# Opening of a diffusion layer on one core: x loaded in half token tiles, the first modulation weights in quarters, and the modulation turned and summed by 128x2 products

## The chip, the cores and the metric

The kernel runs on one core of one Trainium2 chip. The metric is the device time of one execution in microseconds, as the median of several. Engines are named as in the profile: PE is TensorE (its weight loads are PEld), DVE is VectorE, ACT is ScalarE, POOL is GpSimd, SP is the engine that issues most transfers.

## The reference, cut to what matters

The layer normalises 256 latent tokens x and 256 context tokens ctx (D = 2048 channels), modulates them with a scale and a shift that come from a conditioning vector, projects them, and runs neighbourhood attention and a gated linear attention on the projections. What the change touches is the modulation:

```python
mod = jax.nn.silu(c) @ w_mod[l] + b_mod[l]
shift, scale, gate = jnp.split(mod[:, None, :], 3, axis=-1)
mod_c = jax.nn.silu(c_ctx) @ w_mod[l] + b_mod[l]
shift_c, scale_c, gate_c = jnp.split(mod_c, 3, axis=-1)
h = _layer_norm(x) * (1.0 + scale) + shift
h_c = _layer_norm(ctx) * (1.0 + scale_c) + shift_c
aq, ak, av, az, bq, bk, bv, bz, bg, mga, mgb = _split_cols(h @ w_in[l])
```

There are two conditioning vectors (c for the latent tokens, c_ctx for the context), so every channel has two scales and two shifts. All arithmetic is float32; a projection is made of three products of rounded halves (high x high, low x high, high x low).

## The kernel before

The channels are cut into 16 steps kt of 128. The opening (up to about 141 us) makes h for all steps and, at the same time, the projection ak for the first 7 groups of 128 columns (`kps`, `kp2`, names kp0 to kp6). It goes like this:

- SP loads the conditioning vector (cv), four token tiles `rows` of 128 tokens x 2048 channels (1 MB each), and for every step kt the modulation weights `wm{kt}_0` and `wm{kt}_1` (1 MB each; 8 blocks of 128 input channels x 256 outputs, which are 128 scales and 128 shifts) and the key weights `r_ak` (448 KB). `fetch` chains them in this order; `fetch_kt(kt)` issues a step's three. Two steps are fetched at the start, the others from `prepare`, when buffers come free: those of the modulation weights have the tag k8, with 8 buffers.
- PE turns the token tiles (products xt with the identity `ident`, 4 of 128x128 for each evacuation by ACT), and DVE takes mean and variance (`bn_stats`). From these come rsn, and two PE turns and copies make `stat`, with which DVE normalises a step's xt (`normalise`, two instructions).
- `modulate(kt, q)`: 8 products of 32 x 256 per half q, into the PSUM tile gp. The conditioning vectors stand in columns 0 and 1 of 32 (`scp`), and each of the four groups of 32 PSUM partitions collects a quarter of the input channels. So gp holds, in 128 rows, four partial sums of two vectors (rows 32g and 32g + 1) for 256 outputs.
- `activate(kt)`: gp is copied to SBUF (gs; ACT for step 0, DVE for the others), its two halves are turned by PE (L294, into the upper half of gp's bank), so that the outputs lie on the partitions, DVE sums the four groups (the reduction at L297) and adds the bias (L300). The result, `mds`, has a scale and a shift for both token kinds. ACT then makes h rounded (`hl`, L306, two instructions), DVE the same in full precision (h32, L307) and the low half (L308).
- `split_ak` rounds the key weights on ACT (h_ak) and makes their low half on DVE (l_ak, L151).
- Then the 21 kp products of a step: 7 groups x (h_ak with high h, l_ak with high h, h_ak with low h).

A scheduler of the framework sets the order on each engine, from the order of the code, `issue_after` links and its own estimate of times; each engine works through its own list strictly in that order. After the opening, PE goes on with the queries of the first heads (qp), the values and the rest of the layer.

Of the kernel before, what the change touches and what calls it, by code (L numbers as in the profile page):

```python
# [8 lines left out]
F32 = mybir.dt.float32  # L9
# [3 lines left out]
ALU = mybir.AluOpType  # L13
AX = mybir.AxisListType
PSUM = bass.MemoryType.PSUM

P = 128
D = 2048
KT = 16
T = 256  # L20
# [69 lines left out]
def tile_backbone_layer(  # L90
# [21 lines left out]
    nc = tc.nc  # L112
    const = ctx.enter_context(tc.tile_pool(name="const", bufs=1))
# [9 lines left out]
    def k8(shape, name, dt=F32):  # L123
        return work.tile(shape, dt, tag="k8", name=name, bufs=8)
# [4 lines left out]
    def k2(shape, name, dt=F32):  # L129
        return work.tile(shape, dt, tag="k2", name=name, bufs=5)  # L130

    def acc(name):
        return ps.tile([P, 512], F32, tag="acc", name=name, bufs=4)
# [7 lines left out]
    def tiny(shape, name, bufs=4):  # L141
        return small.tile(shape, F32, tag=name, name=name, bufs=bufs)

    def mm(o, a, b, start, stop):
        return nc.tensor.matmul(o, a, b, start=start, stop=stop).ins  # L145
# [24 lines left out]
    ident = const.tile([P, P], F32, name="ident")  # L170
    make_identity(nc, ident)
    rows = hpool.tile([P, 8, D], F32, tag="hl", name="rows")

    def log_exp_after(act):
        with tc.issue_after(act.ins):
            nc.scalar.preload_act_table_set("natural_log_exp_and_others")
# [4 lines left out]
    def fetch(dst, src):  # L181
        with tc.issue_after(queued[-1]) if queued else nullcontext():
            queued.append(nc.sync.dma_start(dst, src).ins)

    def behind(ins):
        return tc.issue_after(ins) if ins is not None else nullcontext()

    wms, raws = {}, {}

    def fetch_kt(kt):  # L190
        wms[kt] = [k8([P, 8, T], f"wm{kt}_{q}") for q in range(2)]
        for q in range(2):
            fetch(wms[kt][q][:], wmod[kt, q])
        raws[kt] = stream.tile([P, 1024], F32, tag="raw", name=f"r_ak_{kt}", bufs=4)
        fetch(raws[kt][:, : P * K0], wak[kt])

# [1 line left out]
    fetch(cv[:], cvec)  # L198
    xts = [k8([P, 4, 512], f"xt{i}") for i in range(4)]
    for i in range(4):  # L200
        fetch(rows[:, i, :], xin[i])
    for kt in range(2):
        fetch_kt(kt)
    bm = const.tile([P, KT, 2, 2], F32, name="bm")
    nc.scalar.dma_start(bm[:], bmod)
    nc.gpsimd.tensor_scalar(bm[:, :, 0, :], bm[:, :, 0, :], 1.0, None, ALU.add)
    sc = const.tile([P, KT, 2], F32, name="sc")
    log_exp_after(nc.scalar.activation(sc[:], cv[:], AF.Sigmoid))
    nc.gpsimd.tensor_tensor(out=sc[:], in0=sc[:], in1=cv[:], op=ALU.mult)
    scp = k2([P, KT, 32], "scp")  # L210
# [20 lines left out]
    for i in range(4):  # L231
        cols = slice(P * i, P * i + P)
        for c in range(4):
            tp = acc(f"xt{i}_{c}")
            for k in range(4):
                kt = 4 * c + k
# [15 lines left out]
    gps, made, pend, last_mm, gs_ins = {}, {}, {}, [None], []  # L252
# [31 lines left out]
    def activate(kt):  # L284
        gp = gps[kt]
        gs = k2([P, T], f"gs{kt}")
        if kt:
            with behind(made[0][1] if kt == 1 else None):
                nc.vector.tensor_copy(gs[:], gp[:, :T])
        else:  # L290
            gs_ins.append(nc.scalar.copy(gs[:], gp[:, :T]).ins)
            split_ak(0)
        for c in range(2):
            t = nc.tensor.transpose(gp[:, T + P * c : T + P * c + P], gs[:, P * c : P * c + P], ident[:])  # L294
        last_mm[0] = t.ins
        md = mds[:, :, :, kt]
        nc.vector.tensor_reduce(  # L297
            md, gp[:, T:].rearrange("p (c g m) -> p c m g", c=2, g=4)[:, :, 0:2, :], AX.X, ALU.add
        )
        nc.vector.tensor_tensor(out=md, in0=md, in1=bm[:, kt], op=ALU.add)  # L300
        h32 = k2([P, 2, T], f"h32_{kt}")
        for s in range(2):
            x = xts[kt // 4][:, kt % 4, T * s : T * s + T]
            m, b = mds[:, 0, s, kt : kt + 1], mds[:, 1, s, kt : kt + 1]
            with behind(pend[0][2] if kt == 0 else None):
                cast = nc.scalar.activation(hhi[:, s, kt, :], x, AF.Identity, scale=m, bias=b)  # L306
            nc.vector.tensor_scalar(h32[:, s, :], x, m, b, ALU.mult, ALU.add)  # L307
        sub = nc.vector.tensor_tensor(  # L308
            out=hlo[:, :, kt, :], in0=h32[:], in1=hhi[:, :, kt, :].bitcast(F32), op=ALU.subtract
        )  # L310
        made[kt] = cast.ins, sub.ins

    def split_ak(kt):
        hi = stream.tile([P, 1024], F32R, tag="hi", name=f"h_ak_{kt}")
        lo = stream.tile([P, 1024], F32R, tag="lo", name=f"l_ak_{kt}")
        n = P * K0
        if kt == 0:
            with behind(gs_ins[0]):
                cast = nc.scalar.copy(hi[:, :n], raws[0][:, :n]).ins
            pend[0] = hi, lo, cast  # L320
            return
        split(hi[:, :n], lo[:, :n], raws[kt][:, :n], made[max(kt - 1, 1)])
        pend[kt] = hi, lo
# [11 lines left out]
    with tc.high_priority(offset=60):  # L335
        normalise(0)
        activate(0)
# [6 lines left out]
    def prepare(kt):  # L344
        if kt + 1 < KT:
            fetch_kt(kt + 1)
        normalise(kt)
        modulate(kt)
        activate(kt)
        split_ak(kt)  # L350

    for kt in range(KT):
# [3 lines left out]
        for p in range(K0):  # L356
# [3 lines left out]
            c = slice(P * p, P * p + P)  # L360
# [244 lines left out]
    for g in range(3):  # L605
        q = k8([P, 2, 2, 2, T], f"q{g}", F32R)
# [13 lines left out]
    q = k8([P, 2, 2, 2, T], "q3", F32R)  # L620
# [284 lines left out]
    for i in range(2):  # L905
        s = slice(4 * i, 4 * i + 4)
# [113 lines left out]
    while steps or waiting:  # L1020
        gate_step()
    log_exp_after(sig)
    tail = hpool.tile([P, 8, D], F32, tag="hl", name="tail")
    fin, gb, zs, zt0 = tail[:, 0:4], tail[:, 4], (tail[:, 5], tail[:, 6]), tail[:, 7]
# [42 lines left out]
    for g in range(NC - 1):  # L1067
        ops = [acc(f"wo{g}_{t}") for t in range(2)]
        for k in range(0, KT, 2):
# [5 lines left out]
            for t in range(2):  # L1075
                for i in range(2):
                    c = slice(512 * i, 512 * i + 512)
# [53 lines left out]
    op = acc("wol_0")  # L1131
# [3 lines left out]
    for i in range(2):  # L1135
        op = acc(f"wol_1{i}")
# [9 lines left out]
    r, q = tiny([P, 1], "rr"), tiny([P, 1], "rt")  # L1146
# [109 lines left out]
```

## Time and profile before

| | |
|---|---|
| time, median of 3 runs | 1223.0 us (1222.77 to 1223.78) |
| the profiled execution | 1226.52 us |
| its span | 1224.8 us, granted clock 0.998 |
| PE busy | 1200.0 us (98%) |
| DVE busy | 772.7 us (63%) |
| ACT busy | 542.6 us (44%) |
| wm transfers | 32 of 1024 KB, 9.1 us from issue to landing (median) |
| r_ak transfers | 16 of 448 KB, 9.4 us |
| rows transfers | 4 of 1024 KB, 8.5 us |

The span is the profiled execution from its first to its last instruction; the device time lies around it. A busy PE is not a PE at its peak: matmuls are pipelined, so a record's duration is longer than its distance to the next. The chain of waits goes back from the last instruction to whatever released it, step by step; only work on it sets the end. The windows give busy time of each engine in a stretch of the span and the share and rate of the 16 transfer engines.

### The profile page before, as it was taken

The page shows a single profiled execution, that of the slowest core. Times are in us where ns is not written, and L with a number is a line of the kernel's source. Part 1 is how long each engine was busy: PE and PEld are TensorE (multiplying, and loading weights), DVE is VectorE, ACT ScalarE, POOL GpSimd, SP SyncE. Part 2 cuts the span into 40 slices and gives each one's busy share as a digit, 9 for nine tenths or more (in the row PEclk, how much of TensorE's full clock was granted, in tenths as well). Part 3 has the DMA queues.
Part 4 walks back from the last instruction along what each step waited for, and adds up shares of the span by engine and source line. Part 5 has one row for each costly group of instructions (what it writes and reads, how often), then busy time and mean ns, then how long its engine had stood idle before and what let it go on. Part 6 is the DMA issues. An engine that isn't in the chain of part 4 may idle for free.

```text
span 1224.8 us, 16303 instructions
## 1 busy us (share of the span) xinstructions
PE 1200.0 (98%) x6233; PEld 991.0 (81%) x6233; DVE 772.7 (63%) x1154; ACT 542.6 (44%) x768; POOL 64.0 (5%) x87
## 2 busy tenths in 40 slices
PE   6999999999999999999999999999999999999997
PEld 5666798989788887888888888888888888888885
DVE  7655677777658676356433376766566665665677
ACT  5322445555545354253533364444444444454340
POOL 1000100000010210002000000000000000000111
PEclk9999999999999999999999999999999999999999
DMA  9998457868632444534445667677676767657661
GB/s 376 417 409 310 133 179 222 260 183 266 226 120 86 138 139 136 190 123 153 158 175 187 220 232 239 230 235 237 240 237 236 238 240 239 231 182 284 222 207 69
DMA packets 77054, 263.45 MB, mean 215 GB/s; under 512 B 8920, under 2 KB 8936, under 8 KB 71856
## 3 DMA queue, kind: packets, MB, share of 16 engines
q1 hardware_dynamic: 73616, 256.69, 60.6%
q0 software_dynamic: 2928, 5.16, 1.8%
q8 instruction: 49, 0.80, 0.3%
q10 hardware_dynamic: 432, 0.56, 0.1%
q14 instruction: 29, 0.24, 0.1%
HBM read 247.66 MB, written 10.52 MB: 211 GB/s over the span
## 4 chain that ended last, share of the span: by engine, by line
PE 78%; DVE 8%; DMA 8%; ACT 3%; issue 2%; POOL 0%; SPq 0%; DVEq 0%; ACTq 0%; POOLq 0%
PE bz L145 7%; PE mgb L145 7%; PE pb L145 7%; PE mga L145 7%; PE o L145 7%; PE g L145 7%; PE kp L145 6%; PE bk L145 5%; PE pa L145 4%; PE bq L145 3%; PE wo L145 3%; PE az L145 3%; PE va L145 2%; DMA sb<-mods 2%; PE gp L145 2%
## 5 line engine op out<-in xcount | busy, mean ns | idle before, releaser
L145 PE MATMUL va<-h_av,hl 128*128 128x352 f32 x384 | 95.7, 325 | 0.9 <-DVE both_aq L391 0.9
L145 PE MATMUL kp<-hl,h_ak 128*128 128x512 f32 x256 | 87.2, 408 | 2.2 <-ACT hl L306 2.2
L151 DVE TENSOR_TENSOR l_wv<-r_wv,h_wv 128x1024 fp32r<-128x1024 f32 x32 | 39.2, 1225 | 72.9 <-ACT h_wv L149 72.8
L145 PE MATMUL o<-h_wv,gt 128*128 128x512 f32 x256 | 83.9, 390 | 0.7 <-ACT gt L149 0.5
L145 PE MATMUL bk<-hl,h_bk 128*128 128x512 f32 x256 | 80.8, 392 | 0.7 <-ACT kf L680 0.7
L145 PE MATMUL bz<-h_bz,hl 128*128 128x512 f32 x256 | 80.7, 392 | 0.0
L145 PE MATMUL mgb<-h_mgb,hl 128*128 128x512 f32 x256 | 79.8, 390 | 0.0
L145 PE MATMUL mga<-h_mga,hl 128*128 128x512 f32 x256 | 79.5, 389 | 0.0
L145 PE MATMUL pb<-h_pb,hl 128*128 128x512 f32 x256 | 79.4, 389 | 0.0
L145 PE MATMUL g<-ah,hr 128*128 128x512 f32 x256 | 79.0, 390 | 0.0
L145 PEld LDWEIGHTS va<-h_av,hl 128*128 128x128 f32 x384 | 67.1, 188 | 2.1 <-DVE both_aq L391 1.2
L149 ACT CAST h_wv<-r_wv 128x1024 fp32r<-128x1024 f32 x32 | 33.6, 1050 | 71.3 <-DMA r_wv<-in_wst 71.3
L151 DVE TENSOR_TENSOR l_pb<-r_pb,h_pb 128x1024 fp32r<-128x1024 f32 x32 | 39.2, 1225 | 39.9 <-ACT h_pb L149 39.9
L145 PEld LDWEIGHTS kp<-hl,h_ak 128*128 128x128 f32 x256 | 48.3, 191 | 19.4 <-issue 4.9
L145 PE MATMUL va<-l_av,hl 128*128 128x352 f32 x192 | 61.7, 321 | 0.0
L151 DVE TENSOR_TENSOR l_mgb<-r_mgb,h_mgb 128x1024 fp32r<-128x1024 f32 x32 | 39.2, 1225 | 30.1 <-ACT h_mgb L149 29.9
L145 PEld LDWEIGHTS o<-h_wv,gt 128*128 128x128 f32 x256 | 48.0, 188 | 11.5 <-ACT gt L149 0.9
L145 PEld LDWEIGHTS bk<-hl,h_bk 128*128 128x128 f32 x256 | 48.1, 188 | 11.3 <-ACT kf L680 1.1
L151 DVE TENSOR_TENSOR l_mga<-r_mga,h_mga 128x1024 fp32r<-128x1024 f32 x32 | 39.2, 1224 | 27.5 <-ACT h_mga L149 27.5
L145 PEld LDWEIGHTS mga<-h_mga,hl 128*128 128x128 f32 x256 | 48.1, 188 | 10.0
L145 PEld LDWEIGHTS pb<-h_pb,hl 128*128 128x128 f32 x256 | 48.1, 188 | 9.9
L145 PEld LDWEIGHTS bz<-h_bz,hl 128*128 128x128 f32 x256 | 48.1, 188 | 9.9
(332 smaller groups left out, 2962.7 us busy)
## 6 DMA issues: line engine op xcount, KB each, us to landing
wm<-in_wmod SPq DMA_DIRECT2D x32, 1024.0 KB, 9.1
hr<-hrows SPq DMA_DIRECT2D x32, 512.0 KB, 4.4
r_wv<-in_wst SPq DMA_DIRECT2D x32, 512.0 KB, 3.6
r_bz<-in_wst SPq DMA_DIRECT2D x32, 512.0 KB, 4.2
wg<-in_wgate SPq DMA_DIRECT2D x64, 256.0 KB, 3.6
r_mga<-in_wst SPq DMA_DIRECT2D x32, 512.0 KB, 4.2
r_mgb<-in_wst SPq DMA_DIRECT2D x32, 512.0 KB, 3.3
r_pb<-in_wst SPq DMA_DIRECT2D x32, 512.0 KB, 3.3
```

Of the source, the lines that this page charges most:

```text
L145: return nc.tensor.matmul(o, a, b, start=start, stop=stop).ins
L149: cast = nc.scalar.copy(hi, src)
L151: sub = nc.vector.tensor_tensor(out=lo, in0=src, in1=hi.bitcast(F32), op=ALU.subtract)
```

## The change

Three edits. The four x transfers become eight of 4 KB rows (half the channels of a token tile each), and the first step's two modulation weight transfers become four. A 128x2 selector `sel` is made once, by a DVE reduction of the identity: its column m has ones in the rows 32g + m. And the two turns of gs against the identity become two products of gs with `sel`, whose results are the two columns of a half already summed over the four groups, so that the reduction on DVE goes and the bias is added straight from PSUM.

```diff
+    sel = const.tile([P, 2], F32, name="sel")
+    nc.vector.tensor_reduce(
+        sel[:], ident[:].rearrange("p (g c) -> p c g", g=4)[:, 0:2, :], AX.X, ALU.add
+    )
...
         for q in range(2):
-            fetch(wms[kt][q][:], wmod[kt, q])
+            for i in range(0, 8, 8 if kt else 4):
+                s = slice(i, i + (8 if kt else 4))
+                fetch(wms[kt][q][:, s], wmod[kt, q][:, s])
...
     for i in range(4):
-        fetch(rows[:, i, :], xin[i])
+        for c in range(0, D, 1024):
+            fetch(rows[:, i, c : c + 1024], xin[i][:, c : c + 1024])
...
         for c in range(2):
-            t = nc.tensor.transpose(gp[:, T + P * c : T + P * c + P], gs[:, P * c : P * c + P], ident[:])
-        last_mm[0] = t.ins
+            t = mm(gp[:, T + 2 * c : T + 2 * c + 2], gs[:, P * c : P * c + P], sel[:], True, True)
+        last_mm[0] = t
         md = mds[:, :, :, kt]
-        nc.vector.tensor_reduce(
-            md, gp[:, T:].rearrange("p (c g m) -> p c m g", c=2, g=4)[:, :, 0:2, :], AX.X, ALU.add
-        )
-        nc.vector.tensor_tensor(out=md, in0=md, in1=bm[:, kt], op=ALU.add)
+        sums = gp[:, T : T + 4].rearrange("p (c m) -> p c m", c=2)
+        nc.vector.tensor_tensor(out=md, in0=sums, in1=bm[:, kt], op=ALU.add)
```

It also moves instructions, since the scheduler orders them anew. First PE, from the turn of step 13 (gp13) to the first half of gp14; a row is a line of the code, the operation, what it writes and reads, its shape, and how many. Before:

```order
L294 MATMUL gp13_1054<-ident_77,gs13_1071 128x128 x2
L145 MATMUL kp45_300<-hl_247,l_ak_12_1022 128x512
L145 MATMUL kp45_300<-hl_247,h_ak_12_1021 128x512 x2
L145 MATMUL kp45_300<-hl_247,l_ak_12_1022 128x512
L145 MATMUL kp45_300<-hl_247,h_ak_12_1021 128x512
L145 MATMUL kp6_301<-hl_247,h_ak_12_1021 128x512
L145 MATMUL kp6_301<-hl_247,l_ak_12_1022 128x512
L145 MATMUL kp6_301<-hl_247,h_ak_12_1021 128x512
L145 MATMUL gp14_1116<-wm14_0_1046,scp_112 32x256 x8
L145 MATMUL kp0_296<-hl_247,h_ak_13_1083 128x512
```

After, on PE, from the pair of step 13 to the same half of gp14:

```order
L145 MATMUL gp13_1049<-sel_83,gs13_1066 128x2 x2
L145 MATMUL kp6_308<-hl_255,l_ak_12_1017 128x512
L145 MATMUL kp6_308<-hl_255,h_ak_12_1016 128x512
L145 MATMUL kp0_303<-hl_255,h_ak_13_1077 128x512
L145 MATMUL kp1_304<-hl_255,h_ak_13_1077 128x512
L145 MATMUL kp2_305<-hl_255,h_ak_13_1077 128x512
L145 MATMUL kp0_303<-hl_255,l_ak_13_1078 128x512
L145 MATMUL kp1_304<-hl_255,l_ak_13_1078 128x512
L145 MATMUL kp2_305<-hl_255,l_ak_13_1078 128x512
L145 MATMUL gp14_1110<-wm14_0_1041,scp_120 32x256 x8
```

Eight products of step 12 and half a gp stood between the turn of step 13 and its first kp product; now two products do, and the half gp stands behind six products of step 13. The second half of a gp has moved behind in the same way. Between the pair and the first kp product of its own step there are now 9 products for kt=9, 5 for kt=10, then 2, 3, 2, 3 and 2 for kt=11 to 15; up to kt=8 there is little change.

DVE in the same step, before:

```order
L289 COPY gs13_1071<-gp13_1054 128x256
L297 TENSOR_REDUCE mds_116<-gp13_1054 128x4
L151 TENSOR_TENSOR l_ak_13_1084<-r_ak_13_988,h_ak_13_1083 128x896
L300 TENSOR_TENSOR mds_116<-mds_116,bm_105 128x4
L307 TENSOR_SCALAR h32_13_1077<-xt3_88,mds_116 128x256 x2
L308 TENSOR_TENSOR hl_247<-h32_13_1077,hl_247 128x2x256
```

After:

```order
L297 COPY gs13_1066<-gp13_1049 128x256
L306 TENSOR_TENSOR mds_124<-gp13_1049,bm_113 128x4
L313 TENSOR_SCALAR h32_13_1071<-xt3_90,mds_124 128x256 x2
L151 TENSOR_TENSOR l_ak_13_1078<-r_ak_13_984,h_ak_13_1077 128x896
L314 TENSOR_TENSOR hl_255<-h32_13_1071,hl_255 128x2x256
```

The reduction is gone, and the low half of the key weights no longer stands between it and the bias but behind h32.

## The prediction

> **What bounds the kernel now.** I read the page first: TensorE (PE) is busy for 98% of the span at a granted clock of 9 tenths or more in all 40 slices, so what counts is idle or added TensorE time.
>
> ```profile
> PE 1200.0 (98%) x6233; PEld 991.0 (81%) x6233; DVE 772.7 (63%) x1154; ACT 542.6 (44%) x768; POOL 64.0 (5%) x87
> ...
> PEclk9999999999999999999999999999999999999999
> ```
>
> The change lies in the opening, before 141 us; there I read the windows, then the chain of waits, then the order of the instructions.
>
> The windows of the opening (columns: stretch, its length, busy time of PE, weight loads, DVE, ACT, POOL, clock, share of the transfer engines, GB/s):
>
> ```profile
> 0.00:10.00 10.00, 3.46 (x17) 3.49 (x18) 3.53 (x7) 4.55 (x6) 3.27 (x13) 1.00 0.79 288
> 10.00:20.00 10.00, 8.70 (x78) 7.63 (x80) 8.66 (x21) 7.23 (x16) 0.00 (x0) 1.00 1.01 424
> 20.00:30.00 10.00, 7.47 (x68) 4.42 (x61) 8.73 (x19) 2.92 (x6) 0.00 (x0) 1.00 1.02 419
> 30.00:40.00 10.00, 9.11 (x66) 5.82 (x68) 7.20 (x14) 4.07 (x7) 0.00 (x0) 1.00 1.02 418
> 120.00:130.00 10.00, 10.00 (x77) 6.03 (x77) 4.26 (x10) 4.08 (x7) 0.20 (x1) 1.00 0.31 106
> ```
>
> To 40 us the transfer engines have no free time and TensorE has some; at 120 us TensorE is full and the transfers are not. The chain of waits (start, length, what) shows where it turns:
>
> ```profile
> 28.25 11.39 DMA r_ak<-in_wak
> 39.74 0.95 ACT h_ak L149
> 40.71 1.09 DVE l_ak L151
> 42.40 0.35 DVE gs L289
> 42.80 0.44 PE gp L294 x2
> 43.23 4.12 PE kp L145 x18
> 47.35 1.86 PE gp L145 x32
> 49.21 0.90 PE kp L145 x3
> 50.11 0.22 PE gp L294 x2
> ```
>
> The landing at 39.64 us is the key weights of step kt=3 (the fourth of its kind on SP). ACT and DVE split it, DVE then copies gs of kt=3, and from the turn at 42.80 us on TensorE never rests: a step is 21 kp products, the two halves of gp and the turn. The same for a late step, and its end:
>
> ```profile
> 110.64 0.22 PE gp L294 x2
> 110.86 1.83 PE kp L145 x8
> 112.69 1.00 PE gp L145 x16
> 113.69 2.52 PE kp L145 x10
> 116.21 1.00 PE gp L145 x16
> 117.21 0.89 PE kp L145 x3
> 118.10 0.22 PE gp L294 x2
> ```
>
> So anything that shortens the time before 42.80 pays only if the landing at 39.64 comes earlier, and anything that costs TensorE time after it is paid in full.
>
> **The change, part by part.**
>
> *Transfers in halves and quarters.* What they start earlier, by the timeline:
>
> ```profile
> 6.43 2.47 DVE L241 BATCH_NORM_STATS2 st<-rows 128x6 f32<-128x512 f32 x4 [6.43 <-DMA rows<-in_xin]
> 23.49 1.42 PE L145 MATMUL kp<-hl,h_ak 128*128 128x512 f32 x5 [1.73 <-ACT hl L306]
> ```
>
> The first x tile (1 MB) starts the statistics at 6.43; its first half is there 0.5 MB / 0.42 = 1.25 us sooner, and DVE has hardly a gap from there to the end of the statistics. Less the new selector reduction in the middle of them (0.2 to 0.4 us: between the 0.18 of the small reduction quoted below and the 0.35 of the gs copy above), the first kp product moves from 23.49 to about 22.5. This reaches the end only through the 39.64. By then must have landed x (4.19 MB) and four steps of 2.10 + 0.46 MB, 14.4 MB together; the windows moved 2.9 + 4.2 + 4.2 + 4.0 = 15.3 MB by 39.64, at full share since 10 us. The transfer waited behind bytes, not for its issue (28.25), so I take no gain. SP now issues six more transfers in the opening, each waiting until the eighth before it is in; with seven halves in flight (3.7 MB, 9 us of work) the engines do not run dry. Rows of 4 KB in place of 8 KB for 6.3 MB can cost: the stretch 10-20 us, all 8 KB rows, made 424 GB/s, the next one, a sixth of it in 3.5 KB rows, 419; if that sixth alone were to blame it ran 7% slower, and 6.3 MB would take 1.1 us more. Other work can explain the 5 GB/s as well: I take 0.2, ends 0 and +1.1. [...]
>
> *Two 128x2 products for two turns, on TensorE.* The turns cost 0.22 a step. No row shows a product with 2 columns. These are f32 products, and the trace has two records with two weight loads for each of those (the 8 of a gp half are x16), against one for a turn. The weight loads by shape (last number before the bar: mean ns):
>
> ```profile
> L145 PEld LDWEIGHTS gp<-wm,scp 128*32 128x32 f32 x512 | 14.2, 109 | 15.8 <-issue 6.2 <-DVE xt L282 0.7 <-DVE xt L281 0.7
> L145 PEld LDWEIGHTS op<-pt,v 128*64 128x64 f32 x128 | 8.7, 137 | 5.3 <-issue 0.7 <-PE kp L145 0.4 <-ACT ga L657 0.4
> L145 PEld LDWEIGHTS ap<-near 128*128 128x128 f32 x64 | 8.4, 191 | 0.3
> ```
>
> From 32 to 128 columns they grow by 82 ns, 0.85 ns a column, so 128 columns occupy 0.109 us whatever is around them. [...] Four loads make 0.43, so +0.21 a step; bounds: the upper one is this, the lower one is a load that is hidden altogether, 0 for the pair, -0.22. I take the load, as the row nearest in shape (128x128 f32). There are 13 pairs from 42.80 on: +2.7 (ends -2.9 and +2.7). [...]
>
> *The reduction leaves DVE.* 16 x 0.18 us, on an engine with 4.26 of 10 us busy: nothing by itself. But it shortens the chain from pair to h. For kt=5, by the timeline:
>
> ```profile
> 49.94 0.38 PE L294 MATMUL gp<-ident,gs 128*128 128x128 f32 x2
> 50.36 0.18 DVE L297 TENSOR_REDUCE mds<-gp 128x4 f32<-128x16 f32 x1 [0.66 <-PE gp L294]
> 50.57 0.17 DVE L300 TENSOR_TENSOR mds<-mds,bm 128x4 f32<-128x4 f32 x1
> 50.77 1.09 ACT L306 ACTIVATE hl<-xt,mds 128x256 fp32r<-128x256 f32 x2 [3.99 <-DVE mds L300]
> 50.77 0.74 DVE L307 TENSOR_SCALAR h<-xt,mds 128x256 f32<-128x256 f32 x2
> 53.84 1.08 DVE L151 TENSOR_TENSOR l_ak<-r_ak,h_ak 128x896 fp32r<-128x896 f32 x1
> ```
>
> From the turn's start (49.94) to h (51.86) is 1.92; less 0.21 for the reduction, plus 0.1 for the longer pair, 1.8 us.
>
> *The order that the scheduler made of it* is the largest term. Before, eight or more kp products and half a gp (1.0 us) stood between the turn of a step and its first kp product, so the 1.92 was covered. Now, from kt=10 on, the second gp half stands late and few are left: 5 products for kt=10, then 2, 3, 2, 3, 2 for kt=11 to 15; everything behind them on TensorE waits for ACT's h. The cover is 0.43 for the pair and 0.23 a product (1.83 for 8): a wait of 1.8 - 0.89 = 0.9 with two, 0.7 with three, 0.2 with five. l_ak now follows h32 on DVE: it ends at 1.8 - 1.1 (ACT) + 0.74 + 1.08 = 2.5 after the pair's start. For kt=12 and 14, with two products ahead of the first that reads it (2.3), another 0.25. Sum: 0.2 + 0.9 + 0.95 + 0.9 + 0.95 + 0.9 = 4.8. One wait of this kind exists today and is replaced, that of kt=15:
>
> ```profile
> 136.07 0.50 PE L145 MATMUL kp<-hl,h_ak 128*128 128x512 f32 x1 [0.51 <-ACT hl L306]
> ```
>
> That leaves +4.3. Ends: each chain 0.3 shorter or longer, some 2.7 and 5.9. The gp halves stand later too, and free their buffers later: at 120 us the transfers have two thirds of their time free, so that costs nothing.
>
> Sum: 0.2 + 2.7 + 4.3 = +7.2 us. The profiled execution took 1226.5 us (span 1224.8), 3.5 above the median of the runs, 1223.0; so 1233.7 for one like it, 1230.2 for the median. I say 1230.
>
> **Rivals.**
> 1. Faster: the opening's gain goes through. If the transfer that lands at 39.64 waited for its issue (behind gp of kt=1), everything after would move by what the first kp gains, 1.0 us; it decides only if pair and waits together cost less than that, and with both at nothing gives 1222.0. The full shares from 10 to 40 us speak against it.
> 2. No change: the loss is taken up by an idle stretch later. TensorE waits about 6 us at 150 us for a transfer:
>
> ```profile
> 147.36 0.61 ACT kn L149
> 147.97 0.69 ACT h_av L149
> 148.69 0.90 DVE l_av L151
> 149.60 5.87 DMA sb<-mods
> ```
>
> If that transfer kept its own time, all 7 us would vanish in it: 1223. But it is issued at the end of l_av, which follows the casts after TensorE's qp products, so it moves along.
> 3. The four loads hide, as the loads of the kp products do, and the pair takes nothing to speak of: 0.2 - 2.9 + 4.3 = +1.6, 1224.6. No row has a product of 2 columns, which speaks for it; that each such product would have to cover 0.109 us speaks against it. [...]
> 4. Slow 4 KB rows: +1.1 in place of 0.2, 1231.1, with the waits at their upper end 1232.7.
>
> **How the numbers follow.** A change under 0.2%, 2.45 us, can't be told from none: the bounds are 1220.6 and 1225.4. Forecast 0.60, all slower. Rival 1: 0.06, faster. Rival 2: 0.10, same. Rival 3: 0.13, its 1224.6 just inside the bound: 0.07 same, 0.06 slower. Rival 4: 0.11, slower. Faster 0.06, same 0.17, slower 0.77. The range leaves out rivals 1 and 2 and a little more: from 1224.0 (rival 3 with somewhat shorter chains) to 1232.7 (rival 4 with long ones).
>
> **What would show it.** In the new trace: the key weights of kt=3 still land at 39.6 to 40.7, and the pair of kt=3 starts near 42.8, though the first kp product starts near 22.5; the pair holds TensorE for 0.4 (0.1 or less by rival 3); five waits of TensorE for ACT's hl, of 0.7 to 0.9 us, between 100 and 146 us; the qp products start near 148.4 in place of 141.4 and all later stretches are as long as before. A landing at 38.5, hl waits below 0.3, or a pair under 0.2 would make it wrong.

## The result, and the profile after

The changed kernel took 1234.3 us in the median of 5 runs (1232.0 to 1236.8), the kernel before, in the same series, 1223.3: ratio 1.0095, 95% interval 1.0083 to 1.0106. In a second series it took 1234.7 us (ratio 1.0091, 1.0077 to 1.0106). It is slower, as forecast, but by 11 to 12 us in place of 7, and outside the range, which ended at 1232.7.

The page of the changed kernel, busy time and granted clock:

```profile
PE 1205.3 (98%) x6265; PEld 993.5 (81%) x6265; DVE 770.5 (63%) x1139; ACT 542.9 (44%) x768; POOL 64.0 (5%) x87
...
PEclk9999999999999999999999999999999999999999
```

The span grew from 1224.8 to 1232.3 us, and TensorE is busy for 5.3 us more. The clock over the whole span is the same (0.998), but not that of the opening. Its windows (columns as in the prediction):

```profile
0.00:10.00 10.00, 3.87 (x19) 3.90 (x20) 3.93 (x7) 4.74 (x7) 3.27 (x13) 1.00 0.77 246
10.00:20.00 10.00, 8.59 (x79) 6.27 (x78) 8.61 (x22) 7.35 (x16) 0.00 (x0) 1.00 1.02 407
20.00:30.00 10.00, 7.66 (x62) 4.34 (x55) 7.64 (x14) 2.70 (x5) 0.00 (x0) 0.83 1.02 420
30.00:40.00 10.00, 8.99 (x65) 6.07 (x64) 6.54 (x14) 3.96 (x6) 0.00 (x0) 1.00 1.02 419
```

In the last column the transfers made 246 and 407 GB/s to 20 us, where it was 288 and 424; from 20 us on the rates are the same.

The third column from the end is the granted clock: 0.83 from 20 to 30 us, where before has 1.00. Read in steps of 2 us, it is 0.50 from 24 to 26 us, with 0.93 and 0.72 on either side: some 3.4 us at half clock. Before has such a stretch too, but behind the opening, at 312 to 316 us:

```profile
310.00:320.00 10.00, 9.05 (x34) 6.54 (x35) 9.54 (x19) 4.80 (x10) 0.00 (x0) 0.83 0.41 133
```

By my estimate, from the clock alone with TensorE busy throughout (2.00 of 2 us in each window from 24 to 28 us), these 3.4 us cost 1.7. Most of the kernels below have such a stretch in the opening: x_wide and x_part are granted 0.83 from 20 to 30 us too, and the longest gp product takes 636 ns in sel_only and after_order and 599 in sel_order, against 404 in before; in low_first it takes 404 as well. What sets it off was not tested. From 43 us to the end of the opening before and after are at full clock, 1.00 in every 2 us.

The chain of waits in the opening:

```profile
2.64 7.58 DMA rows<-in_xin
10.22 0.02 issue
10.24 10.25 DMA wm<-in_wmod
20.49 0.04 issue
20.53 0.68 PE gp L145 x8
21.22 0.02 issue
21.23 0.33 SPq L188
21.56 0.05 issue
21.61 13.77 DMA r_ak<-in_wak
35.38 0.02 issue
...
43.86 0.89 PE kp L145 x3
44.75 0.50 PE gp L145 x4
45.24 4.25 PE kp L145 x18
```

The path now turns at the landing of kt=2's key weights, 35.4 us (33.5 before): from the pair behind it at 37.85 TensorE does not rest until the waits of kt=11. The statistics began at 6.02 us in place of 6.43, but the last of the first step's weights land only at 20.49, and the first kp product came no sooner than before (23.75; before 23.49):

```profile
23.75 2.50 PE L145 MATMUL kp<-hl,h_ak 128*128 128x512 f32 x5 [1.48 <-ACT hl L312]
41.58 0.94 ACT L149 CAST h_ak<-r_ak 128x896 fp32r<-128x896 f32 x1 [1.79 <-DMA r_ak<-in_wak]
```

The second of these rows is ACT's: the key weights of kt=3 are there at 41.5 in place of 39.64, and the pair of kt=3 starts at 44.6 in place of 42.80. Later, TensorE's rows with a wait between 100 and 146 us:

```profile
110.78 0.97 PE L145 MATMUL kp<-hl,h_ak 128*128 128x512 f32 x3 [0.80 <-ACT hl L312]
119.35 0.73 PE L145 MATMUL kp<-hl,h_ak 128*128 128x512 f32 x2 [0.57 <-ACT hl L312]
128.31 0.96 PE L145 MATMUL kp<-hl,h_ak 128*128 128x512 f32 x3 [0.80 <-ACT hl L312]
136.88 0.73 PE L145 MATMUL kp<-hl,h_ak 128*128 128x512 f32 x2 [0.59 <-ACT hl L312]
145.84 0.96 PE L145 MATMUL kp<-hl,h_ak 128*128 128x512 f32 x3 [0.70 <-ACT hl L312]
```

These are the five waits of the prediction. The opening ends where the qp products start. In the instructions of the tile qp (first and last start after the three durations), for before, after, and after in the second series:

```profile
L145 PE MATMUL qp<-hl,h_aq x32: 389/398/403, 141.2 to 152.3; 128*128 128x512 f32 x32
L145 PE MATMUL qp<-hl,h_aq x26: 389/398/403, 150.8 to 159.7; 128*128 128x512 f32 x26
L145 PE MATMUL qp<-hl,h_aq x29: 389/398/403, 150.0 to 160.0; 128*128 128x512 f32 x29
```

So 9.6 and 8.8 us stand at the end of the opening; two executions of one program differ there by 0.8. This first start of qp is the ruler of the experiments. The 0.8 lies ahead of kt=3, whose pair starts at 44.64 and 43.79 us; from there to the qp products the two take 106.1 and 106.2 us. The table has this stretch as well, which the half clock does not touch in before and after.

### The profile page after: what moved, and what is told of

Same layout as the page of the kernel before. It is cut to its first block, busy times and chain, and to the rows that moved or that the text cites. A ratio compares the mean times of both kernels' runs of the same rounds, so it can differ in the third digit from the quotient of the medians.

```text
span 1232.3 us, 16364 instructions
## 1 busy us (share of the span) xinstructions
PE 1205.3 (98%) x6265; PEld 993.5 (81%) x6265; DVE 770.5 (63%) x1139; ACT 542.9 (44%) x768; POOL 64.0 (5%) x87
## 4 chain that ended last, share of the span: by engine, by line
PE 79%; DMA 8%; DVE 7%; ACT 3%; issue 2%; POOL 0%; SPq 0%; DVEq 0%; ACTq 0%; POOLq 0%
PE bz L145 7%; PE mgb L145 7%; PE pb L145 7%; PE mga L145 7%; PE o L145 7%; PE g L145 7%; PE kp L145 7%; PE bk L145 5%; PE pa L145 4%; PE bq L145 3%; PE wo L145 3%; PE az L145 3%; PE gp L145 3%; PE va L145 2%; PE qp L145 2%
## 5 line engine op out<-in xcount | busy, mean ns | idle before, releaser
L312 ACT ACTIVATE hl<-xt,mds 128x256 fp32r<-128x256 f32 x32 | 17.5, 594 | 87.8 <-DVE mds L306 87.7
```

## The experiments

All numbers side by side; before took 1223.1, 1222.9 and 1222.8 us in the three series, and its qp products start at 141.2 us, 98.4 us behind the turn of kt=3.

| kernel | qp starts | later than before | from kt=3's turn or pair to qp | median | ratio, 95% interval |
|---|---|---|---|---|---|
| after (second series) | 150.0 | 8.8 | 106.2 | 1234.7 | 1.0091, 1.0077 to 1.0106 |
| transfers_only | 142.3 | 1.1 | 98.4 | 1224.4 | 1.0008, 0.9999 to 1.0017 |
| sel_only | 149.4 | 8.2 | 106.0 | 1229.9 | 1.0062, 1.0046 to 1.0078 |
| sel_order | 142.9 | 1.7 | 100.0 | 1225.0 | 1.0017, 1.0007 to 1.0028 |
| after_order | 144.5 | 3.3 | 100.0 | 1228.0 | 1.0042, 1.0027 to 1.0058 |
| x_only | 142.5 | 1.3 | 98.2 | 1223.3 | 1.0006, 0.9996 to 1.0016 |
| wm_only | 141.7 | 0.5 | 98.4 | 1223.7 | 1.0007, 0.9999 to 1.0016 |
| x_part | 150.8 | 9.6 | 98.1 | 1233.4 | 1.0081, 1.0067 to 1.0094 |
| x_wide | 142.5 | 1.3 | 98.3 | 1224.1 | 1.0006, 0.9995 to 1.0017 |
| pair_twice | 149.8 | 8.6 | 105.7 | 1231.1 | 1.0069, 1.0052 to 1.0085 |
| low_first | 148.7 | 7.5 | 105.6 | 1231.2 | 1.0071, 1.0053 to 1.0089 |

**The two halves of the change.** transfers_only is before with the transfers of the change:

```diff
-        fetch(rows[:, i, :], xin[i])
+        for c in range(0, D, 1024):
+            fetch(rows[:, i, c : c + 1024], xin[i][:, c : c + 1024])
...
-            fetch(wms[kt][q][:], wmod[kt, q])
+            for i in range(0, 8, 8 if kt else 4):
+                s = slice(i, i + (8 if kt else 4))
+                fetch(wms[kt][q][:, s], wmod[kt, q][:, s])
```

> The kernel before with the x halves and the weight quarters alone; the turns and the reduction stay, and PE's order is that of before. Theory from the two traces: the transfers cost what the key weights of kt=2 and kt=3 land later (1.9 us), so about 1225 us, and the landing of kt=3 at 41.5 in place of 39.6. Rival, the forecast's term: 0.2 us, 1223.5, and the rest of the 11 us is in the pair and the order.

sel_only is before with the selector and its products:

```diff
-            t = nc.tensor.transpose(gp[:, T + P * c : T + P * c + P], gs[:, P * c : P * c + P], ident[:])
+            t = mm(gp[:, T + 2 * c : T + 2 * c + 2], gs[:, P * c : P * c + P], sel[:], True, True)
...
-            md, gp[:, T:].rearrange("p (c g m) -> p c m g", c=2, g=4)[:, :, 0:2, :], AX.X, ALU.add
```

> The changed kernel with the transfers of before (whole x tiles, whole weights); selector products and PE's new order stay. Theory: pair 3.1 us + waits 4.8 us at the end of kp, so about 1231 us. Rival (the transfers are the larger part): under 1228 us.

The transfers alone put the qp products off by 1.1 us, the selector by 8.2; together 9.3, of 8.8 to 9.6 for the whole change. The parts add up. The shift of transfers_only stands ahead of kt=3: like that of before, its chain of waits runs through the landing of kt=3's key weights, and they land 1.1 us later. Of the 8.2 of sel_only 7.6 lie behind kt=3's pair (106.0 against 98.4) and 0.5 ahead of it, where its chain runs over TensorE at half clock: 32 gp products from 26.4 us on take 3.14 us, where before they took 1.91. The order of the instructions is that of before in transfers_only and that of the change in sel_only, so the selector brings the reordering.

**The order taken back.** The kp products are linked behind the halves of gp and behind the pair where the order of before has them; in after_order in the whole change, in sel_order with the transfers of before:

```diff
-            mm(kdst[p], wh[:, c], hhi[:, 0:2, kt, :], kt == 0, False)
...
+            for j in range(3):
+                w, h = (wl if j == 1 else wh)[:, c], (hlo if j == 2 else hhi)[:, 0:2, kt, :]
+                with behind(ahead(kt, 3 * p + j)):
+                    ins = mm(kdst[p], w, h, kt == 0 and j == 0, kt == KT - 1 and j == 2)
```

> The changed kernel whole, with PE's order around gp and the pair as before. Theory: transfers 1.9 + pair 3.1 = 1228.2 us, 5 to 6 us under the changed kernel. Rival (order worth nothing, losses come from the transfers): 1234.

> As sel_only, but kp products are queued behind the gp halves and the pair so that PE's order around them is that of before. Theory: the waits for hl go and the pair alone is left, 13 x 0.24 = 3.1 us: 1226.3. If the loads hid it would be 1222 to 1223.5; if the order of the kp products does not matter, as sel_only.

At the qp products the order is worth 8.2 - 1.7 = 6.5 us without the new transfers, and 9.6 - 3.3 = 6.3 (8.8 - 3.3 = 5.5 by the second execution) with them. Behind kt=3's pair alone it is 6.0 (106.0 - 100.0) and 6.1 to 6.2. In sel_order no row of TensorE has a wait for hl at all, not even that of kt=15 which before has.

**What a pair costs.** pair_twice is sel_order with each pair done twice:

```diff
-        for c in range(2):
+        for c in (0, 1, 0, 1):
             t = mm(gp[:, T + 2 * c : T + 2 * c + 2], gs[:, P * c : P * c + P], sel[:], True, True)
```

> The selector products alone, with the products on TensorE kept in the order of before, and each pair of products done twice (the second time to the same place). Without the doubling the qp products start 1.7 us later than before, 13 steps x 0.13 above the turns' 0.22, so 0.35 a pair. Theory: a pair holds TensorE for 0.35; 13 more of them make +4.5, so +6.2 at the qp products. Rival of the prediction: four weight loads of 0.109 in sequence, 0.44 a pair, +5.7, so +7.4. [...]

The timeline of TensorE, each time the turns or the pair with the kp product behind them: before, sel_order, pair_twice.

```profile
72.16 0.38 PE L294 MATMUL gp<-ident,gs 128*128 128x128 f32 x2
72.29 0.48 PE L145 MATMUL kp<-hl,l_ak 128*128 128x512 f32 x1
```

```profile
72.22 0.50 PE L145 MATMUL gp<-sel,gs 128*128 128x2 f32 x4
72.58 0.47 PE L145 MATMUL kp<-hl,h_ak 128*128 128x512 f32 x1
```

```profile
75.18 0.95 PE L145 MATMUL gp<-sel,gs 128*128 128x2 f32 x8
75.99 0.48 PE L145 MATMUL kp<-hl,h_ak 128*128 128x512 f32 x1
```

From the start of the group to the next kp product: 0.13 us for the turns, 0.36 for a pair, 0.81 for two. The pair costs 0.23 a step over the turns, and the second one adds 0.45, four records of 0.112. That is the size of the weight load that the prediction estimated, 0.109 from the rows of 109 and 191 ns; that it is the load, and not another cost of each record, no run separates. The cost comes with each pair and not once a step. Over the steps the doubling cost 8.6 - 1.7 = 6.9 us, of which 5.7 behind kt=3's pair (105.7 - 100.0): 13 x 0.44, so nearly every step paid. My own expectation of 0.35 for each pair fell too: it divided the 1.7 of sel_order by 13 without seeing that sel_order also gains what before loses at kt=15.

**Which transfers cost.** x_only and wm_only have one of the two splits each (the first and the second piece of the diff of transfers_only). x_part splits x by partitions, x_wide keeps four transfers of 1 MB, but of half rows of two token tiles:

```diff
-        fetch(rows[:, i, :], xin[i])
+        for c in range(0, P, 64):
+            fetch(rows[c : c + 64, i, :], xin[i][c : c + 64, :])
```

```diff
-    for i in range(4):
-        fetch(rows[:, i, :], xin[i])
+    for i in range(0, 4, 2):
+        for c in range(0, D, 1024):
+            fetch(rows[:, i : i + 2, c : c + 1024], xin[i : i + 2, :, c : c + 1024].rearrange("i p c -> p i c"))
```

> Before, with x alone loaded in eight halves of 0.5 MB with 4 KB rows (the modulation weights whole, the turns as before). Both splits together moved the qp products by +1.1 us. Rows theory: the 4 KB rows are slow, each byte of them alike; x has 4.2 of their 6.3 MB, so +0.7 us at the qp products. Size theory: transfers of 0.5 MB at the head of the queue start slowly; then all of it, +1.1. Rival: the split of x costs nothing and the weights' does all, 0. Median 1223.1 to 1224.3, no verdict by the median alone.

> Before, with the modulation weights of the first step alone loaded in halves of each of the two tiles (x whole, the turns as before). Rows theory: 2.1 of the 6.3 MB, +0.35 us at the qp products. Size theory: these stand behind 4.2 MB and the queue is full by then, 0. Rival: the weights do all of it, +1.1. Median 1223.1 to 1224.3.

> Before, with each x tile loaded as two halves of 64 partitions: as many transfers of 0.5 MB as in the change, but with rows of 8 KB. Rows theory: no 4 KB rows, so 0 at the qp products and the first statistics at 6.5 us. Size theory: as with halves by columns, +1.1. Rival: 64 partitions use the transfer engines worse than 128, then more than +1.1, up to 5 us if only half of the engines work on each half.

> Before, with x loaded in four transfers of 1 MB as before, but each takes the left or right half of two token tiles: rows of 4 KB with the number and size of transfers unchanged. With the halves (eight of 0.5 MB, 4 KB rows) the 3 to 6 us window made 298 GB/s in place of 369, and the qp products came 1.3 us late. Rows theory: the 4 KB rows do it; the window makes 300 again and the qp products come about 1.3 late. Size theory: the smaller transfers do it; 370 GB/s and 0.

The windows of the start (GB/s last), in this order: before, x_only, wm_only, x_wide, x_part.

```profile
3.00:6.00 3.00, 0.00 (x0) 0.00 (x0) 0.00 (x0) 1.13 (x1) 1.97 (x6) 1.00 0.93 369
6.00:10.00 4.00, 3.46 (x17) 3.49 (x18) 3.53 (x7) 1.75 (x3) 0.00 (x0) 1.00 1.01 399
```

```profile
3.00:6.00 3.00, 0.07 (x1) 0.10 (x2) 0.18 (x1) 1.12 (x1) 1.96 (x6) 1.00 0.93 298
6.00:10.00 4.00, 4.00 (x20) 4.00 (x21) 3.64 (x7) 2.14 (x4) 0.00 (x0) 1.00 1.02 356
```

```profile
10.00:20.00 10.00, 8.90 (x81) 7.43 (x83) 8.64 (x22) 7.42 (x16) 0.00 (x0) 1.00 1.01 395
```

```profile
3.00:6.00 3.00, 0.00 (x0) 0.00 (x0) 0.00 (x0) 1.25 (x1) 2.08 (x6) 1.00 0.96 318
6.00:10.00 4.00, 2.25 (x10) 1.88 (x11) 2.80 (x5) 1.17 (x2) 0.00 (x0) 1.00 1.03 411
```

```profile
3.00:6.00 3.00, 0.00 (x0) 0.00 (x0) 0.00 (x0) 1.28 (x1) 2.10 (x6) 1.00 0.90 213
6.00:10.00 4.00, 0.72 (x4) 0.75 (x5) 0.76 (x2) 0.00 (x0) 0.00 (x0) 1.00 1.04 219
10.00:20.00 10.00, 7.49 (x39) 6.76 (x38) 5.69 (x11) 4.95 (x9) 0.00 (x0) 1.00 1.02 214
```

From 3 to 10 us before moved 3 x 369 + 4 x 399 = 2703 KB, x_only 2318, x_wide 2598. Small rows in small transfers lose 385 KB, 0.9 us at the steady 420 GB/s, small rows in large transfers 105 KB, 0.25 us; counted from 0 us, where the three made 60, 53 and 36 GB/s, it is 406 and 177 KB. So more than half of the loss of the split x belongs to the 0.5 MB transfers, the rest to the 4 KB rows, by one execution of x_wide. The split weights lose theirs when they come, 395 in place of 424 GB/s from 10 to 20 us, and nearly all of it from 12 to 16 us (377 and 338), in a queue that was full. In transfers_only the same quarters come behind the halves of x and make 408 to 424 from 12 to 20 us (before 420 to 426). So the loss went with the first few small transfers, whether they stood at the head of the queue or not.

The shift of x_only at the qp products is not the price of its transfers alone: from 20.7 us its chain of waits holds no transfer, and TensorE is at half clock for 6.8 us of it (32 gp products at 27.8 us take 3.15 us, where before took 1.91); nor do 1.3 and 0.5 add to the 1.1 of transfers_only. The shift of x_wide says nothing on this either, since two token tiles are now complete only together: its statistics start at 7.0 us and its first kp product at 25.7, 2.2 us late, and from there the chain of waits holds no transfer. Nor did x_part tell rows and sizes apart: 64 partitions moved at half the rate, 213 to 219 GB/s, with the engines marked busy (0.90 from 3 to 6 us, 1.02 to 1.04 from there to 20 us), and the shift was 9.6 us, twice what I had thought the worst case (4.2 MB at 214 in place of 424 GB/s is 9.7 us). It shows another thing: an opening 9.6 us later ends 10.4 us later in the median, so what follows took up nothing of this delay.

**What stands beside the five waits.** low_first is sel_only with l_ak ahead of the copy to gs from step 10 on, and the same number of products between the pair and the wait:

```diff
+        if kt >= 10:
+            split_ak(kt)
         activate(kt)
-        split_ak(kt)
+        if kt < 10:
+            split_ak(kt)
...
-            with behind(made[0][1] if kt == 1 else None):
+            with behind(made[0][1] if kt == 1 else subs[kt] if kt >= 10 else None):
                 nc.vector.tensor_copy(gs[:], gp[:, :T])
```

> The selector products alone, in the order that the scheduler made of them (two or three products between the pair and the first product that needs its h), but from step 10 on DVE splits the key weights (l_ak) ahead of the copy to gs, and no longer between h and its low part. With l_ak in between, the qp products came 8.2 us late, 6.5 of it by the order: 3.5 us of that stand in five waits for ACT's hl, and the other 3 in products that follow at more than 0.23 apart without a wait on record. Theory: these wait for l_ak and for the low part of h, both on DVE; then the five waits stay at 0.6 to 0.8 each and the qp products come 1.5 to 2.5 us earlier, at +5.7 to +6.7. Rival: the rest is something else (the stalled pipeline filling again, the switches to gp); then +8.2 as before.

The waits of TensorE from 98 to 150 us (total, times, longest), sel_only and low_first:

```profile
PE kp L145 <- ACT hl L309: 3.5, 5, 0.8
```

```profile
PE kp L145 <- ACT hl L310: 3.4, 5, 0.8
```

The waits stayed, and the qp products came 0.7 us sooner, of which 0.2 was there ahead of the first of them: 0.5 for l_ak and the low part of h, not 1.5 to 2.5. So this theory holds for a small part only. Where the rest is, a wait's own rows show, here the first of sel_only:

```profile
107.52 0.50 PE L145 MATMUL gp<-sel,gs 128*128 128x2 f32 x4
107.88 0.49 PE L145 MATMUL kp<-hl,l_ak 128*128 128x512 f32 x1
108.20 0.40 PE L145 MATMUL kp<-hl,h_ak 128*128 128x512 f32 x1
109.40 0.96 PE L145 MATMUL kp<-hl,h_ak 128*128 128x512 f32 x3 [0.80 <-ACT hl L309]
110.20 0.86 PE L145 MATMUL kp<-hl,l_ak 128*128 128x512 f32 x3
```

The last product ahead starts at 108.20 and is recorded to 108.60; without the wait the next would have started 0.23 behind it, at 108.43. The row's 0.80 counts from 108.60, so the wait cost 0.97. Five such waits are 3.5 + 5 x 0.17 = 4.3 us. With the 0.5 of DVE's low parts that is 4.8 of the 6.5 which separate sel_only from sel_order. Another 0.5 stands ahead of kt=3 (its pair starts at 43.35 in sel_only and 42.88 in sel_order); part of the other 1.2 lies in the products behind each wait (three from 109.40 to 110.20, 0.80 us, not 0.69), the rest isn't assigned.

**The whole change again**, with the parts:

> The changed kernel once more, in the same series as the parts. Theory: the costs stand at the start of the qp products (before 141.4, after +9.6 us) and are handed down unchanged, so +9.6 there and some 1232.7 in the median. Rival: the stages behind it, which wait for transfers, add to it; then 1234 again, 1.5 above the shift at the qp products.

At the qp products the sum of the parts holds (9.3; 8.8 and 9.6), yet the median is 11.8 above before. The medians put 3.0 us behind the opening (1.4 in the first series); the traces do not show them. From the first qp product to the end of the span before takes 1083.6 us, after 1081.5 and, in the second series, 1083.5. But before's profiled execution stood 3.5 us above its median and had its half clock in this stretch, so the traces are no good ruler here. The waits of TensorE from 370 to 600 us show one place where this kernel loses; after, after in the second series, sel_only, low_first:

```profile
PE o L145 <- ACT gt L149: 1.8, 1, 1.8
```

```profile
PE o L145 <- ACT gt L149: 2.2, 1, 2.2
```

```profile
PE o L145 <- ACT gt L149: 0.8, 1, 0.8
```

```profile
PE o L145 <- ACT gt L149: 2.5, 1, 2.5
```

Before has 0.5, the other kernels 0.4 to 0.7. ACT's rows ahead of it, in after and in sel_only:

```profile
481.13 1.05 ACT L149 CAST h_wv<-r_wv 128x1024 fp32r<-128x1024 f32 x1 [2.87 <-DMA r_wv<-in_wst]
```

```profile
480.11 1.05 ACT L149 CAST h_wv<-r_wv 128x1024 fp32r<-128x1024 f32 x1 [1.79 <-DMA r_wv<-in_wst]
```

The transfer of r_wv is issued at 475.5 us in both and takes 1 us more in after, and what follows it on ACT comes late. That is 1.3 to 1.7 us more than before in the two executions of this kernel that were profiled; but low_first, whose median is only 0.9 above its shift, has the longest of these waits, so it is no mark of the whole change. In low_first and in the second execution of after another stretch at half clock follows it, from 484 to 488 us (the longest o product takes 793 and 792 ns); in the first execution of after none does (499 ns, and a granted clock of 1.00 from 484 to 488). Why the transfer takes longer there was not shown.

## Why the prediction was right or wrong, point by point

- **No gain from the opening: right.** The first kp product did not even come sooner: I had counted on 1 us from the halved first x tile. The statistics started 0.4 us sooner and ended 0.15 sooner, with 0.2 for the selector's reduction in their midst, and the last of the first step's weights landed at 20.49. Rival 1 was out for a stronger reason than I gave.
- **Rival 2, the loss is taken up at 150 us: wrong, as forecast.** x_part's delay of 9.6 us at the qp products is 10.4 in the median. My reading was wrong all the same: TensorE does not wait 6 us there. It is busy for 5.57 of the 6 us from 150 to 156 and waits 0.88 at 156.45, for DVE; in after that wait is gone.
- **Transfers, +0.2: mis-sized, 1.1** by transfers_only. This is the upper end and rival 4's value, but not by its mechanism: a steady 7% on 4 KB rows was not the cost. I looked at the queue while 1 MB transfers ran; the loss stands in the first few of the small ones, with the engines marked as busy as before (0.93 from 3 to 6 us in both before and x_only).
- **The pair, +2.7: near in size, its mechanism not shown.** It cost 13 x 0.23 = 3.0, 0.3 above the upper end. The pair holds TensorE for 0.36 and the turns for 0.13, where I had 0.43 and 0.22; the difference held. That four weight loads of 0.109 stand uncovered was my estimate, and no run shows that it is the loads that cost; what pair_twice shows is the price of each record, 0.112. Rival 3 is out.
- **The order, +4.3: the mechanism right, the size a little low, and partly by luck.** Net it cost 7.6 - 3.0 = 4.6 behind kt=3's pair in sel_only, and 4.7 in after (106.1 - 98.4 - 3.0). The five waits for hl were there, with pair to hl at 1.83 us (108.90 to 110.73; 1.8 forecast). Counted by starts they make 4.3 (forecast 0.9 or 0.7 each, 4.1 together), and l_ak and the low part of h 0.5 (forecast 0.5). Two errors nearly cancel. I put nothing for what else follows a wait, 1.2 us (6.0 - 4.8) that is only in part located. And I priced the wait that was replaced, that of kt=15, by its recorded 0.51, which counts from the modelled end of the product ahead: sel_order, where it is gone, is only 1.6 to 1.7 late with 3.0 us of pairs in it, so it cost some 1.3 to 1.4.
- **The sum at the qp products:** forecast +7.2, measured 9.6 and 8.8. Ahead of kt=3 it is 1.8 and 1.0, where I had 0.2; from there on 7.7 and 7.8, where I had 7.0.
- **"All later stretches are as long as before": not borne out by the medians, and open.** 9.6 and 8.8 at the qp products became 11.0 and 11.8 in the medians. The wait at 483 us is 1.3 to 1.7 longer than before in both traces of after, yet these traces are not longer behind the opening. The medians of the other kernels stand from 1.3 below to 1.7 above their shifts at the qp products, so a tenth of a per cent behind the opening can't be assigned with this ruler.
- **The steps that failed.** The median was missed by 3.8 us in the first series and 4.6 in the second. 1.6 and 0.8 of it stand ahead of kt=3: the transfers' term was taken from a steady queue, 0.2 where transfers_only has 1.1, and nothing else was put ahead of 42.80 us, where the two executions differ by 0.8. 0.7 and 0.8 are the pairs and the order. 1.4 and 3.0 lie behind the qp products, where the prediction put nothing; their cause stays open.

## What to carry to other kernels

Before halving a transfer, ask what is waiting for the first half: here it started one engine 0.4 us sooner and cost the whole queue 1.1. A product with few columns can cost much more than its columns suggest (here 0.112 us for each record of 128x2, against 0.23 from one 128x512 product to the next), and a shorter instruction list on a side engine can lead a scheduler to put the dependent product closer behind; read the new order at every place where a chain through three engines was covered, and count the cover in products. A wait in the timeline counts from the modelled end of the product ahead (0.80 in sel_only, where it cost 0.97): for its price, take the distance of starts less the usual distance. Before a shift between two traces is put down to an edit, read the granted clock of both in short windows.

## What the runs showed of the hardware that I had not expected

- In x_part the transfers to 64 partitions went at 214 to 219 GB/s from 6 to 20 us, where those to 128 partitions made 399 to 424 before, although the engines' busy share was 1.02 to 1.04. In the packet records of x_part an 8 KB packet of x took 608 ns, where it took 309 before, both in the median.
- The 4 KB packets of x cost little in the median, 159 ns each in after, 318 for two, 3% over the 309 of one of 8 KB before; but in the mean they took 186 in after and 189 in x_only, where one of 8 KB took 334 before. The first small transfers were the slow ones: 298 in place of 369 GB/s from 3 to 6 us in x_only, 338 in place of 426 from 14 to 16 us in wm_only.
- The f32 products of 128x2 are two records each, with two weight loads (in pair_twice 8 of both for four products), and the second pair there adds 0.45 us, 0.112 a record; the four records of a single pair in sel_order hold TensorE for 0.36.
- TensorE's granted clock fell to half for stretches of 3.4 us, and not at the same place: from 24 us on in after (0.50 from 24 to 26), from 312 us on in before (0.59 and 0.56 in the two windows to 316). TensorE was in part idle just ahead of both, busy for 0.52 of the 2 us from 22 to 24 us in after and for 1.05 of those from 310 to 312 us in before. Yet before had 0.51 of 2 us from 22 to 24 us and kept the full clock, 1.00 to 312 us; what brings the stretch about was not shown.
